# In-product transposes and projections, and a PSUM-seeded last block product, in the final stage of a decoder trunk

## The chip, the cores and the metric

The kernel runs on one core of one Trainium2 chip. The metric is the device time of one execution in microseconds (us), lower is better. The time before is 1259.64 us, the median of three runs (1259.33 to 1259.81).

The core's engines, as the profile names them: PE (TensorE, matrix products and transposes; PEld is its weight load), DVE (VectorE), ACT (ScalarE), POOL (GpSimd) and SP (SyncE, which here only issues DMAs). Each engine works through its own queue of instructions in order. SBUF is the working memory; PSUM holds the results of PE in eight banks of 128 x 512 f32 values.

## The reference

Two decoder layers over 512 tokens of width 1024. Each ends with a per-layer embedding, and the change lies in that of the second layer, the last stage of the whole computation:

```python
def _per_layer_embedding(x, p_i, norm, w_gate, w_proj):
    gate = jax.nn.sigmoid(_rms_norm(x, norm) @ w_gate)
    return gate * (p_i @ w_proj)
...
        x = x + _conv_ffn(_rms_norm(x, ffn_norm[i]), ffn_w_up[i], ffn_conv_w[i], ffn_conv_b[i], ffn_w_down[i])
        x = x + _per_layer_embedding(x, p[i], ple_norm[i], ple_w_gate[i], ple_w_proj[i])
    return x
```

Here `w_gate` is 1024 x 1024, `p_i` is 512 x 256 and `w_proj` is 256 x 1024. All values are float32.

## The kernel before

**Layout.** The residual `x` is held transposed, as eight tiles `xT[m]` of 128 channels x 512 tokens. Products in float32 accuracy are made of three passes of a reduced form: each operand is split into a high and a low part, and high x high, high x low and low x high are added up in a PSUM bank (`mm3`, L156 to L158, and in the last stage L889 to L891). ACT makes the high part with a copy (L100, L136, L868) and DVE the low part with a subtraction (L101, L137, L869).

**PSUM.** Two groups of four banks: `ps` (for the large products) and `pa` (for everything small: transposes, projections, norm sums). Tiles are handed out from a pool, and a tile's bank is free again when its last reader is done.

**Order of work.** A planner orders the instructions of each engine by readiness and program order. Inside `tc.manual_schedule(...)`, in `ple1`, the instructions of PE, DVE and ACT keep the order in which they are written.

**The last stage.** `ffn(1, ...)` ends with the down projection. For each of its eight output tiles `done` adds the residual (L767), and `blocks` (L254) prepares, for pairs of tiles, the left operands of the next product: the gate product of `x` (512 x 1024) with `w_gate` (1024 x 1024) is done as a two-by-two block product with seven block products instead of eight, so `blocks` forms sums and differences of the blocks of `x` (`e1`, `o1`, `o2`, `s1` to `s4`), and `minus` (L875) forms differences of the weight blocks `b11`, `b12`, `b22`, `b21`. The squares of `x` are summed into `acc` (L248 to L252). `end_norm` (L290) turns `acc` into the scale `r` per token: four small matmuls against ones (L296), a DVE step (`rs`, L165) and a power on POOL (L166).

`ple1` (L843) then runs the block products in the order e1, s1, s2, s3, s4, o2, o1. One block product (`add`, L880) is 24 matmuls: 4 blocks j of the inner dimension x 2 token tiles i x 3 passes, into two banks. The banks `X` hold e1, then e1 + s2, then e1 + s2 + s3 and so on; `Q` holds s1, later s1 + s4. Values that are needed again later are copied to SBUF by ACT (`ka`: the result of e1; `kd`: s1; `kb`: e1 + s2) and added by DVE when a quadrant of the result is complete (`summed`, L925). `chunk` (L861) splits a half of a weight block into its high and low part for `add`; the names are wt1, wt2, wt3, wt4, w22, w21 and, for `w_proj`, wj.

For each quadrant of the output (a pair of token tiles t by a column half hf) there are three steps outside the block products:

- `back(hf, t)` (L893): four PE transposes of `xT` into a `pa` bank, and an ACT copy to SBUF;
- `proj(t, w)` (L908): six matmuls p x w_proj into a `pa` bank;
- `finish(hf, t, ...)` (L930): ACT takes the sigmoid, scaled by `r`, of the gate (L933), DVE multiplies it with the projection in its `pa` bank (L934) and adds the residual (L935), and SP issues the store (L936).

These steps stand between the block products: before s2, after s2, after s3, after s4 and after o2. In the last product, o1, the three result banks (one whole token tile and two halves of the other) are each summed with `ka` by DVE before the sigmoid (L995 to L1005).

The weights and `p` of this stage are loaded by DMAs on SP's queue while the down projection still runs.

Of the kernel before, what the change touches and what calls it, by code (L numbers as in the profile page):

```python
# [13 lines left out]
AF = mybir.ActivationFunctionType  # L14
# [7 lines left out]
NT = S // P  # L22
# [33 lines left out]
class Kernel:  # L56
# [658 lines left out]
    def ffn(self, i, next_gain):  # L715
        nc, a, tc = self.nc, self.a, self.tc
        xg, R = self.xg, None
        wu = a["ffn_w_up"][i].rearrange("(k p) n -> p k n", p=P)
        w0, w1, w2, bb = self.fcv
        with tc.tile_pool(name=f"ffn{i}", bufs=1) as fp:  # L720
            acts = [self.pair(self.fp, "b0", "b1") for f in range(8)]
            for f in range(8, NF, 2):
                four = self.four(fp)
                acts += [(four[:, 0], four[:, 1]), (four[:, 2], four[:, 3])]

            def taps(ps, f):
                y = fp.tile([P, S], F32, tag="zt", name=self.nm("zt"), bufs=4)
                z = fp.tile([P, S + 2], F32, tag="z", name=self.nm("z"), bufs=3)
                nc.gpsimd.memset(z[:, :2], 0.0)
                nc.vector.tensor_tensor(z[:, 2:], ps, R, ALU.mult)  # L730
                nc.scalar.activation(y, z[:, 2:], AF.Identity, scale=w2[:, f : f + 1], bias=bb[:, f : f + 1])  # L731
                for tap, w in ((1, w1), (0, w0)):
                    nc.vector.scalar_tensor_tensor(  # L733
                        out=y, in0=z[:, tap : tap + S], scalar=w[:, f : f + 1], in1=y, op0=ALU.mult, op1=ALU.add
                    )
                return y

            for d in range(NF // 2):
                wg = self.weights(wu[:, :, 256 * d : 256 * d + 256], ND, 256)
                wv = self.weights(wu[:, :, DFF + 256 * d : DFF + 256 * d + 256], ND, 256)  # L740
                for c in range(2):
                    f = 2 * d + c
                    got = []
                    pss = []
                    for w in (wg, wv):
                        ps = self.ps()
                        for k in range(ND):
                            self.mm3(ps, w(k, c * P, (c + 1) * P), xg[k], start=k == 0, stop=k == ND - 1)
                        pss.append(ps)
                    if R is None:  # L750
                        R = self.spread()
                    for w, ps, fo in ((wg, pss[0], f), (wv, pss[1], NF + f)):
                        y = taps(ps, fo)
                        if w is wg:
                            nc.scalar.activation(y, y, AF.Gelu)  # L755
                        got.append(y)
                    g, y = got
                    nc.vector.tensor_tensor(y, g, y, ALU.mult)  # L758
                    self.split(acts[f], y)
            self.begin_norm(("a0", "a1"))  # L760
            done = self.residual(next_gain)
            if i == 1:
                self.forms = []
                scratch = lambda: fp.tile([P, S], F32, tag="zt", name=self.nm("gx"), bufs=4)

                def done(m, ps):
                    nc.vector.tensor_tensor(self.xT[m], self.xT[m], ps, ALU.add)  # L767
                    self.blocks(m, next_gain, scratch)

            self.project(self.rows(a["ffn_w_down"][i]), acts, ND, done)  # L770
            self.end_norm()
            if i == 1:
                self.ple1(fp)

    def p_halves(self, i):
# [67 lines left out]
    def ple1(self, fp):  # L843
# [1 line left out]


        nc, a, tc = self.nc, self.a, self.tc
        r, forms = self.r, self.forms
        wg = a["ple_w_gate"][1].rearrange("(j u p) n -> u p j n", p=P, u=2)
        wp = a["ple_w_proj"][1].rearrange("(k p) n -> p k n", p=P)  # L850
        sl = lambda hl, t: (hl[0][:, t * P : (t + 1) * P], hl[1][:, t * P : (t + 1) * P])
        H, J = D // 2, ND // 2
# [8 lines left out]
        def chunk(src):  # L861
            if count[0] % 6 < 3:
                h, l = (self.wp.tile([P, 2, H], F32R, tag=g, name=self.nm(g), bufs=3) for g in ("wh", "wl"))
            else:
                four = self.four(fp)
                h, l = four[:, :2], four[:, 2:]
            count[0] += 1
            nc.scalar.activation(h, src, AF.Copy)  # L868
            nc.vector.tensor_tensor(l, src, h.bitcast(F32), ALU.subtract)  # L869
            return h, l  # L870

        def chunks(raw):
            return [chunk(raw[:, 2 * q : 2 * q + 2, :]) for q in range(2)]

        def minus(out, x, y):  # L875
            for q in range(2):
                c = slice(2 * q, 2 * q + 2)
                nc.vector.tensor_tensor(out[:, c, :], x[:, c, :], y[:, c, :], ALU.subtract)  # L878
# [46 lines left out]
        def summed(g, kept):  # L925
            s = result()[:, : g.shape[1]]
            nc.vector.tensor_tensor(s, g, kept, ALU.add)
            return s

        def finish(hf, t, g, x, pj, s=None, c0=0, c1=H):  # L930
            if s is None:
                s = result()[:, c0:c1]
            nc.scalar.activation(s, g, AF.Sigmoid, scale=r[:, t : t + 1])  # L933
            nc.vector.tensor_tensor(s, s, pj[:, c0:c1], ALU.mult)  # L934
            nc.vector.tensor_tensor(s, s, x[:, c0:c1], ALU.add)  # L935
            nc.sync.dma_start(self.out[0, t * P : (t + 1) * P, hf * H + c0 : hf * H + c1], s)  # L936

        ET = mybir.EngineType
        b11 = block(0, 0, True)
# [4 lines left out]
        wj_raw = self.four(fp, F32)  # L944
# [2 lines left out]
        proj_load(0)  # L947
        minus(b11, b12, b11)
        wt1 = [chunk(b11[:, :2, :])]
        X = [self.ps() for _ in range(2)]  # L950
        with tc.manual_schedule(engines={ET.PE, ET.DVE, ET.Activation}):
            add(X, "e1", w11, first=True)
            wt1.append(chunk(b11[:, 2:, :]))
            minus(b11, b22, b11)
            ka = [self.sp.tile([P, S], F32, tag=g, name=self.nm("keep"), bufs=n) for g, n in (("acc", 1), ("sq", 2))]
            for k, x in zip(ka, X):
                nc.scalar.copy(k, x)
            pT = self.load_p(1, fp, pin)
            wt2 = chunks(b11)
            wj = chunk(wj_raw[:, 2:, :])  # L960
            Q = [self.ps() for _ in range(2)]
            add(Q, "s1", wt1, first=True)
            minus(b12, b22, b12)
            kd = keep(Q, "R")
            wt3 = chunks(b12)
            xs = [back(1, t) for t in (2, 3)]
            add(X, "s2", wt2)
            kb = [self.sp.tile([P, S], F32, tag="sq", name=self.nm("keep"), bufs=2), result()]
            for k, x in zip(kb, X):
                nc.scalar.copy(k, x)  # L970
            pjs = [proj(t, wj) for t in (2, 3)]
            w22 = chunks(b22)
            minus(b11, b21, b11)
            wt4 = [chunk(b11[:, :2, :])]
            add(X, "s3", wt3)
            ss = [summed(X[t], kd[t]) for t in (0, 1)]
            for t in (0, 1):
                finish(1, t + 2, ss[t], xs[t], pjs[t], ss[t])
            xs = [back(1, t) for t in (0, 1)]
            pjs = [proj(t, wj) for t in (0, 1)]  # L980
            wt4.append(chunk(b11[:, 2:, :]))
            wj = chunk(wj_raw[:, :2, :])
            add(Q, "s4", w22)
            ss = [summed(Q[t], kb[t]) for t in (0, 1)]
            for t in (0, 1):
                finish(1, t, ss[t], xs[t], pjs[t], ss[t])
            xs = [back(0, t) for t in (2, 3)]
            pjs = [proj(t, wj) for t in (2, 3)]
            w21 = chunks(b21)
            add(X, "o2", wt4)  # L990
            for t in (0, 1):
                finish(0, t + 2, X[t], xs[t], pjs[t])
            xs = [back(0, t) for t in (0, 1)]
            pjs = [proj(t, wj) for t in (0, 1)]
            Y = [self.ps() for _ in range(3)]  # L995
            halves = ((0, H // 2), (H // 2, H))

            add(None, "o1", w21, first=True, order=[(j, 0, (0, H), Y[0]) for j in range(J)])
            s = summed(Y[0], ka[0])
            finish(0, 0, s, xs[0], pjs[0], s)  # L1000
            for y, c in zip(Y[1:], halves):
                y = y[:, : H // 2]
                add(None, "o1", w21, first=True, order=[(j, 1, c, y) for j in range(J)])
                s = summed(y, ka[1][:, c[0] : c[1]])
                finish(0, 1, s, xs[1], pjs[1], s, *c)  # L1005


    def mixer1(self):
# [450 lines left out]
```

## Time and profile before

| What | Value |
|---|---|
| Median of three runs | 1259.64 us |
| The profiled execution, whole | 1259.64 us |
| Its span in the profile | 1257.8 us |
| Instructions | 14849 |
| Mean granted clock of TensorE | 0.998 |
| Start of e1, first matmul of the last stage | 1191.20 us |
| First matmul of s1 / s2 / s3 / s4 / o2 / o1 | 1198.89 / 1205.24 / 1213.50 / 1226.47 / 1236.55 / 1245.82 us |
| Start of the last matmul | 1251.29 us |
| End of the last add on DVE | 1255.21 us |

Times in the profile count from the start of the span; what lies between the span and the whole time (1.84 us) is outside it. A row of a timeline gives the start, the duration, the engine, the line of the kernel, the operation, output <- inputs by their names, shapes and, in brackets, how long the engine sat idle before it and who released it. Rows with xN are several instructions of one kind in a row. Matmuls overlap, so the time that each takes of PE is the distance between starts and not the listed duration. The granted clock is 1.00 at full speed.

### The profile page before, as it was taken

The page shows a single profiled execution, that of the slowest core. Times are in us where ns is not written, and L with a number is a line of the kernel's source. Part 1 is how long each engine was busy: PE and PEld are TensorE (multiplying, and loading weights), DVE is VectorE, ACT ScalarE, POOL GpSimd, SP SyncE. Part 2 cuts the span into 40 slices and gives each one's busy share as a digit, 9 for nine tenths or more (in the row PEclk, how much of TensorE's full clock was granted, in tenths as well). Part 3 has the DMA queues.
Part 4 walks back from the last instruction along what each step waited for, and adds up shares of the span by engine and source line. Part 5 has one row for each costly group of instructions (what it writes and reads, how often), then busy time and mean ns, then how long its engine had stood idle before and what let it go on. Part 6 is the DMA issues. An engine that isn't in the chain of part 4 may idle for free.

```text
span 1257.8 us, 14849 instructions
## 1 busy us (share of the span) xinstructions
PE 1240.0 (99%) x5809; PEld 1031.0 (82%) x5809; DVE 800.6 (64%) x1230; ACT 559.2 (44%) x864; POOL 54.8 (4%) x150
## 2 busy tenths in 40 slices
PE   7999999999999999999999999999999999999997
PEld 7877788888888888888989988888888888888876
DVE  6786556777777633346779665557777777344584
ACT  6466344444444322234564544435444444233362
POOL 2500000000000000000100000000000000000000
PEclk9999999999999999999999999999999999999999
DMA  6221332223332222232322212233333222333401
GB/s 212 74 96 49 89 101 79 90 100 101 101 101 101 92 92 92 92 101 92 108 73 66 89 46 74 94 109 101 101 101 100 88 85 97 101 102 107 167 17 51
DMA packets 111002, 117.42 MB, mean 93 GB/s; under 512 B 2728, under 2 KB 106210, under 8 KB 110932
## 3 DMA queue, kind: packets, MB, share of 16 engines
q1 hardware_dynamic: 109568, 115.35, 27.9%
q0 software_dynamic: 560, 0.42, 0.2%
q8 instruction: 45, 0.74, 0.2%
q10 hardware_dynamic: 804, 0.70, 0.2%
q14 instruction: 25, 0.20, 0.1%
HBM read 114.37 MB, written 2.10 MB: 93 GB/s over the span
## 4 chain that ended last, share of the span: by engine, by line
PE 91%; DVE 4%; ACT 2%; issue 2%; POOL 1%; DMA 1%; SPq 0%; DVEq 0%; ACTq 0%; POOLq 0%
PE ps L156 27%; PE ps L157 27%; PE ps L158 27%; PE pa L1179 1%; PE pa L156 1%; DMA xin<-in_x_dram 1%; PE pa L1293 1%; PE pa L157 1%; PE pa L158 0%; DVE wl L137 0%; DVE raw L878 0%; PE pa L1270 0%; PE pa L541 0%; POOL rq L166 0%; PE pa L588 0%
## 5 line engine op out<-in xcount | busy, mean ns | idle before, releaser
L136 ACT ACTIVATE wh<-raw 128x1024 fp32r<-128x1024 f32 (+4 forms) x212 | 214.4, 1013 | 349.0 <-PE ps L157 300.3
L137 DVE TENSOR_TENSOR wl<-raw,wh 128x1024 fp32r<-128x1024 f32 (+4 forms) x212 | 246.7, 1165 | 160.6 <-ACT wh L136 159.6
L156 PE MATMUL ps<-a,wh 128*128 128x512 f32 x864 | 337.1, 390 | 0.0
L157 PE MATMUL ps<-a,wh 128*128 128x512 f32 x864 | 336.7, 390 | 0.0
L158 PE MATMUL ps<-a,wl 128*128 128x512 f32 x864 | 336.5, 389 | 0.0
L156 PEld LDWEIGHTS ps<-a,wh 128*128 128x128 f32 x864 | 162.2, 188 | 34.1 <-issue 0.7
L157 PEld LDWEIGHTS ps<-a,wh 128*128 128x128 f32 x864 | 162.3, 188 | 33.9 <-issue 0.3
L158 PEld LDWEIGHTS ps<-a,wl 128*128 128x128 f32 x864 | 162.2, 188 | 33.6
L733 DVE SCALAR_TENSOR_TENSOR zt<-z,vfa,zt 128x512 f32<-128x512 f32 x176 | 131.4, 749 | 3.6 <-ACT zt L731 0.6
L156 PE MATMUL ps<-b,wh 128*128 128x512 f32 x320 | 126.5, 396 | 0.5 <-ACT b L100 0.5
L158 PE MATMUL ps<-b,wl 128*128 128x512 f32 x320 | 125.3, 392 | 0.0
L157 PE MATMUL ps<-b,wh 128*128 128x512 f32 x320 | 125.0, 391 | 0.0
L730 DVE TENSOR_TENSOR z<-ps,R 128x512 f32<-128x512 f32 x88 | 60.4, 688 | 74.7 <-PE ps L158 74.7
L157 PE MATMUL ps<-four,wh 128*128 128x512 f32 x224 | 87.2, 389 | 0.0
L156 PE MATMUL ps<-four,wh 128*128 128x512 f32 x224 | 87.2, 389 | 0.0
L158 PE MATMUL ps<-four,wl 128*128 128x512 f32 x224 | 87.2, 389 | 0.0
L731 ACT ACTIVATE zt<-z,vfb 128x512 f32<-128x512 f32 x88 | 70.8, 807 | 5.1 <-DVE z L730 3.3
L156 PEld LDWEIGHTS ps<-b,wh 128*128 128x128 f32 x320 | 60.0, 188 | 13.9 <-ACT b L100 1.3
L158 PEld LDWEIGHTS ps<-b,wl 128*128 128x128 f32 x320 | 60.1, 188 | 12.5
L157 PEld LDWEIGHTS ps<-b,wh 128*128 128x128 f32 x320 | 60.1, 188 | 12.2
L755 ACT ACTIVATE zt<-zt 128x512 f32<-128x512 f32 x44 | 27.8, 631 | 74.8 <-DVE zt L733 74.8
L100 ACT ACTIVATE four<-zt 128x512 fp32r<-128x512 f32 x28 | 17.7, 632 | 77.4 <-DVE zt L758 77.4
(347 smaller groups left out, 1566.5 us busy)
## 6 DMA issues: line engine op xcount, KB each, us to landing
raw<-in_ffn_w_up_dram SPq DMA_DIRECT2D x44, 1024.0 KB, 5.0
raw<-in_ffn_w_down_dram SPq DMA_DIRECT2D x16, 1024.0 KB, 5.1
raw<-in_hy_w_in_dram SPq DMA_DIRECT2D x8, 1024.0 KB, 4.9
raw<-in_gla_w_in_dram SPq DMA_DIRECT2D x8, 1024.0 KB, 5.3
raw<-in_ffn_w_down_dram SPq DMA_DIRECT2D x8, 768.0 KB, 4.3
raw<-in_ple_w_gate_dram SPq DMA_DIRECT2D x6, 1024.0 KB, 5.1
raw<-in_gla_w_out_dram SPq DMA_DIRECT2D x4, 1024.0 KB, 5.1
raw<-in_gla_w_in_dram SPq DMA_DIRECT2D x4, 672.0 KB, 4.0
```

The source lines that it names most:

```text
L100: nc.scalar.activation(h, src, AF.Copy)
L136: nc.scalar.activation(hv, v, AF.Copy)
L137: nc.vector.tensor_tensor(lv, v, hv.bitcast(F32), ALU.subtract)
L156: mm(out, lh, rh, start=start, stop=False)
L157: mm(out, lh, rl, start=False, stop=False)
L158: mm(out, ll, rh, start=False, stop=stop)
L730: nc.vector.tensor_tensor(z[:, 2:], ps, R, ALU.mult)
L731: nc.scalar.activation(y, z[:, 2:], AF.Identity, scale=w2[:, f : f + 1], bias=bb[:, f : f + 1])
L733: nc.vector.scalar_tensor_tensor(out=y, in0=z[:, tap : tap + S], scalar=w[:, f : f + 1], in1=y, op0=ALU.mult, op1=ALU.add)
L755: nc.scalar.activation(y, y, AF.Gelu)
L1179: mm(second(pl[:, c], b), F[:, c], second(F[:, c], b), start=True, stop=True)
L1293: mm(po, sc[:, c], vt[j][:, h * GDV : (h + 1) * GDV], start=True, stop=j == 0)
```

## The change

The norm of the second layer's embedding moves from the end of `ffn` into the hand-written order, behind the first two steps of s1. The transposes and projections move into the block products: s1, s2, s4 and o2 are cut in two parts, and `back` and `proj` run between the parts (for o1: between its first bank and its two halves). wj is prepared behind wt3 instead of ahead of s1. A sigmoid of `r` with an unused result stands ahead of s3. In the last product, ACT copies `ka` into the PSUM banks that o1 will use (parts of `Q` and `X`, no banks of their own any more), o1's matmuls add to what is there, and the sigmoid reads the bank; the three DVE sums are gone. `self.r` is read in `finish` where `r` was.

```diff
@@ ffn
             self.project(self.rows(a["ffn_w_down"][i]), acts, ND, done)
-            self.end_norm()
-            if i == 1:
+            if i == 0:
+                self.end_norm()
+            else:
                 self.ple1(fp)
...
@@ ple1, finish
-            nc.scalar.activation(s, g, AF.Sigmoid, scale=r[:, t : t + 1])
+            nc.scalar.activation(s, g, AF.Sigmoid, scale=self.r[:, t : t + 1])
...
-        X = [self.ps() for _ in range(2)]
+        X, Q = [[self.ps() for _ in range(2)] for _ in range(2)]
+        both = (0, H)
         with tc.manual_schedule(engines={ET.PE, ET.DVE, ET.Activation}):
             add(X, "e1", w11, first=True)
             wt1.append(chunk(b11[:, 2:, :]))
             minus(b11, b22, b11)
+            steps = [(j, i, both, Q[i]) for j in range(J) for i in range(2)]
+            add(None, "s1", wt1, first=True, order=steps[:2])
+
+            self.end_norm()
             ka = [self.sp.tile([P, S], F32, tag=g, name=self.nm("keep"), bufs=n) for g, n in (("acc", 1), ("sq", 2))]
             for k, x in zip(ka, X):
                 nc.scalar.copy(k, x)
+            wt2 = chunks(b11)
             pT = self.load_p(1, fp, pin)
-            wt2 = chunks(b11)
-            wj = chunk(wj_raw[:, 2:, :])
-            Q = [self.ps() for _ in range(2)]
-            add(Q, "s1", wt1, first=True)
+            add(None, "s1", wt1, order=steps[2:])
             minus(b12, b22, b12)
             kd = keep(Q, "R")
             wt3 = chunks(b12)
+            wj = chunk(wj_raw[:, 2:, :])
+            steps = [(j, i, both, X[i]) for j in range(J) for i in range(2)]
+            add(None, "s2", wt2, order=steps[:4])
             xs = [back(1, t) for t in (2, 3)]
-            add(X, "s2", wt2)
+            add(None, "s2", wt2, order=steps[4:])
...
             wt4 = [chunk(b11[:, :2, :])]
+            nc.scalar.activation(self.few(NT, "rlo"), self.r, AF.Sigmoid)
             add(X, "s3", wt3)
             ss = [summed(X[t], kd[t]) for t in (0, 1)]
             for t in (0, 1):
                 finish(1, t + 2, ss[t], xs[t], pjs[t], ss[t])
+            steps = [(j, i, both, Q[i]) for j in range(J) for i in range(2)]
+            add(None, "s4", w22, order=steps[:6])
             xs = [back(1, t) for t in (0, 1)]
             pjs = [proj(t, wj) for t in (0, 1)]
             wt4.append(chunk(b11[:, 2:, :]))
             wj = chunk(wj_raw[:, :2, :])
-            add(Q, "s4", w22)
+            add(None, "s4", w22, order=steps[6:])
             ss = [summed(Q[t], kb[t]) for t in (0, 1)]
+
+            halves = ((0, H // 2), (H // 2, H))
+            Y = [Q[0]] + [y[:, : H // 2] for y in (Q[1], X[0])]
             for t in (0, 1):
                 finish(1, t, ss[t], xs[t], pjs[t], ss[t])
+            nc.scalar.copy(Y[0], ka[0])
+            nc.scalar.copy(Y[1], ka[1][:, : H // 2])
+            steps = [(j, i, both, X[i]) for j in range(J) for i in range(2)]
+            add(None, "o2", wt4, order=steps[:6])
             xs = [back(0, t) for t in (2, 3)]
             pjs = [proj(t, wj) for t in (2, 3)]
             w21 = chunks(b21)
-            add(X, "o2", wt4)
+            add(None, "o2", wt4, order=steps[6:])
             for t in (0, 1):
                 finish(0, t + 2, X[t], xs[t], pjs[t])
+                if t == 0:
+                    nc.scalar.copy(Y[2], ka[1][:, H // 2 :])
+            add(None, "o1", w21, order=[(j, 0, both, Y[0]) for j in range(J)])
             xs = [back(0, t) for t in (0, 1)]
             pjs = [proj(t, wj) for t in (0, 1)]
-            Y = [self.ps() for _ in range(3)]
-            halves = ((0, H // 2), (H // 2, H))
-
-            add(None, "o1", w21, first=True, order=[(j, 0, (0, H), Y[0]) for j in range(J)])
-            s = summed(Y[0], ka[0])
-            finish(0, 0, s, xs[0], pjs[0], s)
+            finish(0, 0, Y[0], xs[0], pjs[0])
             for y, c in zip(Y[1:], halves):
-                y = y[:, : H // 2]
-                add(None, "o1", w21, first=True, order=[(j, 1, c, y) for j in range(J)])
-                s = summed(y, ka[1][:, c[0] : c[1]])
-                finish(0, 1, s, xs[1], pjs[1], s, *c)
+                add(None, "o1", w21, order=[(j, 1, c, y) for j in range(J)])
+                finish(0, 1, y, xs[1], pjs[1], None, *c)
```

More of the change, by code (lines that the diff above doesn't have):

```diff
@@ L847, in ple1 @@
         nc, a, tc = self.nc, self.a, self.tc
-        r, forms = self.r, self.forms
+        forms = self.forms
         wg = a["ple_w_gate"][1].rearrange("(j u p) n -> u p j n", p=P, u=2)
```

## The prediction

> **What bounds the kernel now.** I read the page first: the busy shares and the chain that ended last.
>
> ```profile
> PE 1240.0 (99%) x5809; PEld 1031.0 (82%) x5809; DVE 800.6 (64%) x1230; ACT 559.2 (44%) x864; POOL 54.8 (4%) x150
> PE 91%; DVE 4%; ACT 2%; issue 2%; POOL 1%; DMA 1%; SPq 0%; DVEq 0%; ACTq 0%; POOLq 0%
> ```
>
> TensorE (PE) is the bound, so only time in which PE stands still or runs slowly, and time after its last matmul, can be won. The diff touches only the end of the kernel, so next come busy times by stretch there.
>
> ```profile
> 1196.60:1251.40 54.80, 51.65 (x253) 42.98 (x252) 36.76 (x43) 26.14 (x36) 1.92 (x1) 0.97 0.08 30
> ...
> 1219.00:1222.00 3.00, 0.98 (x9) 0.74 (x7) 1.50 (x3) 2.70 (x4) 0.00 (x0) 1.00 0.00 0
> 1222.00:1225.50 3.50, 3.42 (x8) 2.75 (x9) 3.43 (x6) 2.77 (x4) 0.00 (x0) 0.51 0.33 130
> ```
>
> Columns: stretch, length, busy PE, PEld, DVE, ACT, POOL, then the granted clock, DMA share and GB/s. From the end of product e1 to the last matmul is 54.8 us. Within it PE does little for 3 us at 1219, and for the 3.5 us after that its clock is 0.51. The waits of PE in the stage, and its own timeline, say why:
>
> ```profile
> PE pa L156 <- DVE so L934: 2.8, 2, 2.1
> PE pa L296 <- DVE acc L252: 0.4, 1, 0.4
> ```
>
> ```profile
> 1196.41 0.39 PE L891 MATMUL ps<-wh,b 128*128 128x512 f32 x1
> 1197.15 1.05 PE L296 MATMUL pa<-ones,acc 128*128 128x1 f32 x8 [0.35 <-DVE acc L252]
> 1198.07 1.07 PE L795 MATMUL pa<-cf,pin 128*128 128x128 f32 x8
> 1198.89 0.48 PE L889 MATMUL ps<-wh,a 128*128 128x512 f32 x1
> ...
> 1218.94 1.04 PE L897 MATMUL pa<-cf,xT 128*128 128x128 f32 x8
> 1222.08 0.79 PE L156 MATMUL pa<-wh,four 128*128 128x512 f32 x1 [2.09 <-DVE so L934]
> ...
> 1226.47 0.40 PE L889 MATMUL ps<-four,a 128*128 128x512 f32 x1
> ...
> 1233.68 0.50 PE L156 MATMUL pa<-wh,four 128*128 128x512 f32 x1 [0.70 <-DVE so L934]
> ...
> 1251.29 0.28 PE L891 MATMUL ps<-four,b 128*128 128x256 f32 x1
> ```
>
> Back-to-back matmuls start 0.2265 us apart (23 steps from 1213.50 to 1218.71 in product s3); their listed 0.39 overlaps. PE loses four times: (a) e1's last slot ends at 1196.64, and the norm's matmuls start at 1197.15: 0.51. (b) At 1218.94 the eight transposes of two `back` take a mean 0.885 (the two clean groups: 1204.45 to 1205.24, 1241.99 to 1242.97), so PE is free at 1219.83 and starts the projection at 1222.08: 2.25. It needs a `pa` bank, of which there are four, and the one whose turn it is holds the projection that finish(1, 2) multiplies at L934. (c) The 12 matmuls of that projection then take 4.39 (1222.08 to 1226.47) against 12 x 0.2265 = 2.72: 1.67 for the low clock. (d) The same bank wait again, 1232.83 to 1233.68: 0.85. Together 5.28.
>
> The tail, from the timelines of DVE and ACT:
>
> ```profile
> 1250.94 0.69 DVE L935 TENSOR_TENSOR so<-so,xt 128x512 f32<-128x512 f32 x1
> 1251.55 0.42 DVE L927 TENSOR_TENSOR so<-ps,keep 128x256 f32<-128x256 f32 x1
> ...
> 1252.54 0.42 DVE L934 TENSOR_TENSOR so<-so,pa 128x256 f32<-128x256 f32 x1 [0.57 <-ACT so L933]
> 1253.00 0.42 DVE L935 TENSOR_TENSOR so<-so,xt 128x256 f32<-128x256 f32 x1
> 1253.34 0.42 DVE L927 TENSOR_TENSOR so<-ps,keep 128x256 f32<-128x256 f32 x1
> 1253.79 0.51 ACT L933 ACTIVATE so<-so,rtok 128x256 f32<-128x256 f32 x1 [1.28 <-DVE so L927]
> 1254.33 0.42 DVE L934 TENSOR_TENSOR so<-so,pa 128x256 f32<-128x256 f32 x1 [0.57 <-ACT so L933]
> 1254.79 0.42 DVE L935 TENSOR_TENSOR so<-so,xt 128x256 f32<-128x256 f32 x1
> ```
>
> The last matmul starts at 1251.29, but its sum (L927) starts only at 1253.34, behind the previous half's multiply and add in DVE's queue. The last add ends at 1255.21: 3.92 after the last matmul's start; the store takes the rest of the span.
>
> **The change, part by part.** The sum is made for PE from 1196.64 on; all matmuls and transposes stay, only their order changes.
>
> Norm behind six matmuls of s1. They need wt1[0], ready at 1193.80, and run 1196.64 to 1198.00; `acc` is ready at 1197.10, so wait (a) goes: -0.51. Norm (0.92, to 1198.92), p transposes (0.82, to 1199.74) and 18 matmuls of s1 (0.09 for the first after a transpose, 0.32 against 0.23, and 4.08) end at 1203.91. The norm's release of `acc` comes 0.85 later, and ACT's two keeps (0.96) with it, to 1200.05.
>
> Order of wj. DVE is full here and wj's low part is now last. From 1197.61: wt1 1.13, two subtractions 2.27, rs 0.08, wt2 2.27, pT 1.20, two subtractions 2.27, wt3 2.27, wj 1.22, all from the rows of before, end at 1210.3. ACT's part of each fits in front (wt2's first: 1200.05 + 1.05 = 1201.10, DVE is there at 1201.09). PE: s2's 12, two `back` (0.885), 0.09, s2's 12 reach the projection at 1210.32. Bounds: 0 if DVE is as quick as that, 0.8 if its seven changes of partner each cost another 0.1 (a dependent start trails its releaser by 0.03 to 0.1 in the timelines). I take 0.2, near the low end because most of DVE's operations wait for nothing.
>
> Transposes and projection after 18 of s4's 24 matmuls. With s3 from 1213.2 to 1218.7, the 18 run to 1222.74, the transposes to 1223.6, and only then is the `pa` bank wanted. It comes free with L934: s3's first bank is done about 1218.2, then sum 0.69, sigmoid 0.73, multiply 0.69 and starts between: 1220.5. So 3.1 us of cover; (b) and with it (c) go: -2.25 - 1.67. The same after 18 of o2 (bank wanted 1232.8, free about 1230.2): -0.85. In o1 it is wanted at 1240.6 and free at 1237.9.
>
> Sigmoid on r ahead of s3. It pulls the table load (1.28 in before, on the path behind the sum) into ACT's 1.94 us of idle time before it: 1.28 + 0.21 (a 128x4 activation) fits. Without that cover the multiply is late by under 1.3, inside the 3.1 above. Nothing extra.
>
> Weights prepared later in ACT's and DVE's queues: wt4[1] ready about 1226.5, used at 1230.5; w21's halves ready 1235.5 and 1236.7, used at 1236.9 and 1238.3. If that 1.4 is used up, o1 waits one for one.
>
> Seeds in PSUM: three ACT copies replace three DVE sums. No row of before has ACT writing PSUM; bounds are a 128x128 ACT operation reading it (0.36) and the 128x1024 one in SBUF (1.06); I take the 0.61 of the 128x512 copy out of PSUM. The first two come about 1230, behind them wait the copies of the `back` at 1232.3, so 2 us hide them even at 1.06 each. Matmuls that add to a bank have the same 0.2265 as those that start one (s2 against s1).
>
> Tail: the last half goes from matmul to sigmoid without a sum. Matmul 0.28, start 0.04, then the steps of before from sigmoid to add: 1252.00 to 1252.54, to 1253.00, + 0.42 = 1.42. So 1.74 instead of 3.92: -2.18. The first half's add is over by then, 0.5 before.
>
> PE's total: 180 x 0.2265 = 40.77, 24 halves x 0.1196 = 2.87, norm 0.92, p 0.82, four pairs of `back` 3.54, five first matmuls 0.45, wj 0.2: 49.57 against 54.77, -5.2. The queue of stores on SP only moves up. With the tail -7.4: span 1257.8 - 7.4 = 1250.4. The profiled execution took 1259.64 (1.84 around the span), which is the median, so **1252.2 us**.
>
> [...]
>
> **Rivals.**
> B, the planner's order: norm and its `rs` leave the part in front of the hand-written order, so block DVE work (wt1 and two subtractions, 3.4 us) could be placed ahead of the last `acc` add. Then `acc` is ready at 1200.5, PE stands 2.5 us after its six matmuls, and as at (b) the clock falls: +1.67, less the 0.2 at wj: 1256.2. For: ACT's half of wt1 already ran early, at 1192.14. Against: DVE was full up to 1197.61 with older work.
> C, the tail keeps its length: finish(0, 0) is late and its multiply and add stand before the halves. +2.2: 1254.4. Against: sigmoid by 1242, multiply and add by 1243.5, the first half's sum only at 1244.9.
> D, no gain: each of the five transpose groups inside a product costs 1.5 us more than its 0.885, by waits for banks or weights that I have hidden: 1259.6. Against: covers of 1.4 to 3.1.
> [...]
>
> **How the numbers follow.** My forecast 0.74, B 0.10, C 0.05, D 0.04, E 0.07. A change under 0.2% (2.5 us) is about what can't be told from none; A, B and C are faster by more: 0.89, D is the same: 0.04, E slower: 0.07. The range runs from 1250.9 (wj free, `back` at 0.79 each time, and 0.7 of starts saved) to B's 1256.2.
>
> **What would show it.** Right: PE's six L889 to L891 before L296 without a wait; no wait for L934; clock 1.00 throughout; the last add 1.7 after the last matmul's start; first sigmoid without the table load. Wrong: a wait of L156 for L869 above 0.8 at about 1210, any stretch near clock 0.5, or a wait in front of the norm.

## The result and the profile after

The changed kernel takes 1251.93 us (median of 6 runs, 1251.36 to 1252.46) against 1259.59 us before (6 runs, 1259.33 to 1259.81). The ratio is 0.9939, 95% interval 0.9927 to 0.9952: faster by 7.7 us, and the forecast was 1252.2. The span of the profiled execution is 1250.0 us in place of 1257.8.

The changed kernel's page, its busy shares and its chain that ended last:

```profile
PE 1237.4 (99%) x5809; PEld 1029.8 (82%) x5809; DVE 799.0 (64%) x1227; ACT 560.8 (45%) x868; POOL 55.0 (4%) x150
PE 94%; DVE 2%; issue 1%; ACT 1%; POOL 1%; DMA 1%; SPq 0%; DVEq 0%; POOLq 0%
```

PE has as many instructions as before; its share of the chain went from 91% to 94%, DVE's from 4% to 2%: what was won is time in which PE waited for others. The busy times by stretch, columns as before:

```profile
1196.60:1246.50 49.90, 49.37 (x253) 41.55 (x251) 37.12 (x44) 28.64 (x42) 1.93 (x1) 1.00 0.10 38
1219.00:1222.00 3.00, 3.00 (x15) 2.49 (x14) 2.82 (x5) 1.12 (x2) 0.00 (x0) 1.00 0.07 27
1222.00:1225.50 3.50, 3.50 (x22) 2.97 (x21) 0.46 (x2) 2.31 (x4) 0.00 (x0) 1.00 0.36 131
```

The stretch at 1219, where PE did 0.98 us of work in 3, is full, and the one after it, at clock 0.51 before, is at 1.00. The changed kernel's timeline of PE shows where the moved work went, and where the one new wait is:

```profile
1197.71 0.39 PE L892 MATMUL ps<-wh,a 128*128 128x512 f32 x1
1197.94 0.95 PE L296 MATMUL pa<-ones,acc 128*128 128x1 f32 x8
1198.74 1.07 PE L796 MATMUL pa<-cf,pin 128*128 128x128 f32 x8
1199.57 0.48 PE L890 MATMUL ps<-wh,a 128*128 128x512 f32 x1
...
1210.10 0.39 PE L156 MATMUL pa<-wh,four 128*128 128x512 f32 x1
1210.40 0.50 PE L157 MATMUL pa<-wl,four 128*128 128x512 f32 x1
...
1222.55 1.03 PE L898 MATMUL pa<-cf,xT 128*128 128x128 f32 x8
1223.34 0.48 PE L156 MATMUL pa<-wh,four 128*128 128x512 f32 x1
```

The norm (L296) starts right behind six matmuls of s1, with no wait in brackets. The transposes inside s4 take 0.79, and the projection follows them at once (L156 at 1223.34). At 1210.10 a projection starts and its second matmul, the first to read wj's low part, is 0.07 late and the third another 0.11: the new wait, 0.18.

The end of the kernel, from its timeline over all engines:

```profile
1245.69 0.28 PE L892 MATMUL ps<-four,b 128*128 128x256 f32 x1
...
1246.01 0.47 ACT L934 ACTIVATE so<-ps,rtok 128x256 f32<-128x256 f32 x1 [0.96 <-PE ps L892]
1246.52 0.42 DVE L935 TENSOR_TENSOR so<-so,pa 128x256 f32<-128x256 f32 x1 [0.55 <-ACT so L934]
1246.97 0.42 DVE L936 TENSOR_TENSOR so<-so,xt 128x256 f32<-128x256 f32 x1
```

The sigmoid reads the bank as soon as the last matmul is out, and the last add ends 1.70 us after that matmul's start, against 3.92 before.

### The profile page after: what moved, and what is told of

The parts are those of the page before. It is cut to its first block, busy times and chain, and to the rows that moved or that the text cites. A ratio compares the mean times of both kernels' runs of the same rounds, so it can differ in the third digit from the quotient of the medians.

```text
span 1250.0 us, 14845 instructions
## 1 busy us (share of the span) xinstructions
PE 1237.4 (99%) x5809; PEld 1029.8 (82%) x5809; DVE 799.0 (64%) x1227; ACT 560.8 (45%) x868; POOL 55.0 (4%) x150
## 4 chain that ended last, share of the span: by engine, by line
PE 94%; DVE 2%; issue 1%; ACT 1%; POOL 1%; DMA 1%; SPq 0%; DVEq 0%; POOLq 0%
PE ps L156 28%; PE ps L158 27%; PE ps L157 27%; PE pa L1192 1%; PE ps L892 1%; PE ps L890 1%; PE ps L891 1%; PE pa L157 1%; PE pa L1306 1%; PE pa L156 1%; PE pa L158 1%; DMA xin<-in_x_dram 1%; DVE wl L137 0%; PE pa L1283 0%; PE pa L541 0%
## 5 line engine op out<-in xcount | busy, mean ns | idle before, releaser
L156 PE MATMUL ps<-a,wh 128*128 128x512 f32 x864 | 336.9, 390 | 0.0
L156 PEld LDWEIGHTS ps<-a,wh 128*128 128x128 f32 x864 | 162.2, 188 | 33.9 <-issue 0.7
L156 PE MATMUL ps<-b,wh 128*128 128x512 f32 x320 | 126.5, 396 | 0.5 <-ACT b L100 0.5
L156 PE MATMUL ps<-four,wh 128*128 128x512 f32 x224 | 87.1, 389 | 0.0
L156 PEld LDWEIGHTS ps<-b,wh 128*128 128x128 f32 x320 | 60.0, 188 | 13.9 <-ACT b L100 1.3
```

What stands on the lines that cost most here:

```text
L156: mm(out, lh, rh, start=start, stop=False)
```

## The experiments

Single times of one kernel differ by one to two us, because the work ahead of the last stage does: e1 started between 1190.67 and 1192.69 in the profiles of these runs. Inside the last stage the profiles agree to some hundredths, so the readings rest on two lengths: **stage**, from e1's first matmul to the start of the last matmul, and **tail**, from there to the end of the last add. The medians stand beside them (before, run beside them: 1259.41, 1259.57 and 1259.51 in the three batches). "Wait" is PE's wait for a `pa` bank behind s3.

| Kernel | stage | tail | wait | clock after it | median, ratio to before (95%) |
|---|---|---|---|---|---|
| before | 60.09 | 3.92 | 2.09 | half | 1259.59 |
| after | 54.56 | 1.70 | none | full | 1251.93, 0.9939 (0.9927 to 0.9952) |
| sigmoid_early_alone | 57.25 | 3.94 | 0.76 | full | 1256.31, 0.9977 (0.9968 to 0.9986) |
| seeds_alone | 58.52 | 1.70 | 2.09 | full | 1256.60, 0.9983 (0.9973 to 0.9992) |
| sums_ahead | 60.16 | 2.53 | 2.09 | half | 1257.93, 0.9990 (0.9981 to 1.0000) |
| inserts_alone | 54.61 | 2.55 | none | full | 1253.10, 0.9953 (0.9938 to 0.9968) |
| no_early_sigmoid | 54.57 | 1.70 | none | full | 1252.32, 0.9943 (0.9928 to 0.9958) |
| s4_whole | 55.55 | 1.71 | 0.70 | full | 1252.33, 0.9944 (0.9927 to 0.9960) |
| s4_whole_no_sigmoid | 58.47 | 1.70 | 2.04 | half | 1256.17, 0.9973 (0.9964 to 0.9983) |
| norm_first | 55.08 | 1.70 | none | full | 1252.36, 0.9945 (0.9930 to 0.9960) |
| wait_longer_by_3 | 56.03 | 1.70 | 1.17 | full | 1252.77, 0.9946 (0.9933 to 0.9960) |
| wait_longest | 56.17 | 1.70 | 1.33 | full | 1253.96, 0.9956 (0.9942 to 0.9969) |
| seeds_and_sigmoid | 57.23 | 1.69 | 0.72 | full | 1254.73, 0.9961 (0.9946 to 0.9976) |
| smaller_last_piece | 56.30 | 1.33 | none | full | 1253.64, 0.9954 (0.9941 to 0.9966) |

### The wait behind s3: the early sigmoid alone

Before, with one line:

```diff
+            nc.scalar.activation(self.few(NT, "rlo"), self.r, AF.Sigmoid)
             add(X, "s3", wt3)
```

> The kernel before with one line added: the unused sigmoid of r ahead of s3. Theory: the table load (1.28 us) leaves the path from the sum of s3 to the multiply that frees the bank, so PE's wait after s3 falls from 2.25 to about 0.95; as the wait of 0.85 after s4 left the clock at full speed, this one does too, and the 1.67 us of half clock goes: 1259.6 - 1.3 - 1.7 = 1256.6. Rival: any wait at this place lets the clock fall, so only the load is won: 1258.3. Second rival: the table load is paid elsewhere on the path: 1259.6.

The stage shortened by 2.84. Waits of PE in this kernel's last stage:

```profile
PE pa L156 <- DVE so L934: 1.5, 2, 0.8
PE pa L296 <- DVE acc L252: 0.4, 1, 0.4
```

The two waits for a bank are 1.5 us together in place of 2.8, the longer one 0.76, and the clock stayed at full speed behind it. So the table load (1.28 us in before) was on the path, and the low clock was a consequence of it: a wait of 0.76 did not bring it, one of 2.09 can. The rival that any wait lowers the clock falls, and so does the one that the load is paid elsewhere on the path.

### The wait behind s3: s4 uncut, with and without the early sigmoid

After, with back and proj between s3 and s4 again; the second kernel also leaves out the line of the early sigmoid:

```diff
-            add(None, "s4", w22, order=steps[:6])
             xs = [back(1, t) for t in (0, 1)]
             pjs = [proj(t, wj) for t in (0, 1)]
...
-            add(None, "s4", w22, order=steps[6:])
+            add(None, "s4", w22, order=steps)
```

> The changed kernel with back and proj of token tiles 0 and 1 between s3 and s4 again, s4 uncut; the early sigmoid stays. Theory: PE waits about 0.9 us for the bank (back done at 1219.3, multiply done at 1220.2), and that is too short to lower the clock: 1251.9 + 0.9 = 1252.8. Rival: the clock falls for any wait here: +2.6, 1254.5.

> As s4_whole, and without the early sigmoid: the place as it was before the change, all else changed. Theory: wait 2.2 and half clock for 3.4 us again: 1251.9 + 2.2 + 1.7 = 1255.8, granted clock near 0.5 after the wait. Rival: the wait without the low clock: 1254.1.

Against after, the stages are 0.99 and 3.91 longer; 0.9 and 3.9 were expected. The second one's busy times (1221.90 to 1226.00) and its PE timeline:

```profile
1221.90:1226.00 4.10, 3.60 (x10) 2.90 (x11) 4.03 (x6) 3.19 (x5) 0.00 (x0) 0.66 0.34 127
```

```profile
1222.40 0.50 PE L156 MATMUL pa<-wh,four 128*128 128x512 f32 x1 [2.04 <-DVE so L935]
1222.73 0.39 PE L157 MATMUL pa<-wl,four 128*128 128x512 f32 x1
1222.96 0.42 PE L158 MATMUL pa<-wh,four 128*128 128x512 f32 x1
1223.19 0.61 PE L156 MATMUL pa<-wh,four 128*128 128x512 f32 x1
1223.61 0.63 PE L157 MATMUL pa<-wl,four 128*128 128x512 f32 x1
```

The wait of 2.04 is back and so is the low clock (0.66 on average here), but not at once: after the wait two matmuls still follow each other at 0.23, and only from 1223.19 on are they 0.42 apart. In these profiles either the early sigmoid or the cut of s4 by itself removes the low clock; the cut also removes what is left of the wait.

### The early sigmoid where s4 is cut

After, with that one line left out.

> The changed kernel without the unused sigmoid of r. Theory: the table load goes back behind the sum of s3, the multiply that frees the bank is 1.3 us later (about 1221.5), still ahead of the projection inside s4 at 1223.3, so nothing changes: 1251.9, no wait of PE there. Rival: the load delays the path of s4 after all: 1253.2.

Stage 54.57 against 54.56, no wait of PE: with s4 cut, the line is worth nothing. The two edits overlap, and the gains of edits that are tried one at a time on before must not be added.

### The tail: the seeds alone, and the order of DVE alone

Before with the seeds of o1 (Y in parts of Q and X, three ACT copies, matmuls that add, no sums), the transposes and projections left between the products:

```diff
-            add(None, "o1", w21, first=True, order=[(j, 0, (0, H), Y[0]) for j in range(J)])
-            s = summed(Y[0], ka[0])
-            finish(0, 0, s, xs[0], pjs[0], s)
+            add(None, "o1", w21, order=[(j, 0, (0, H), Y[0]) for j in range(J)])
+            finish(0, 0, Y[0], xs[0], pjs[0])
...
-                s = summed(y, ka[1][:, c[0] : c[1]])
-                finish(0, 1, s, xs[1], pjs[1], s, *c)
+                finish(0, 1, y, xs[1], pjs[1], None, *c)
```

> The kernel before with only the last product seeded in PSUM (three ACT copies, no DVE sums in o1), transposes and projections between the products as before. Theory: the tail from the last matmul's start to the last add shortens from 3.92 to about 1.74 us and nothing else changes: 1259.6 - 2.2 = 1257.4. Rival: without the transposes and projections inside o1, finish(0, 0) still stands in DVE's queue ahead of the halves, so only the sum itself (0.4 to 0.5) and part of the queue is won: 1258.3 to 1259.1.

And before with nothing but another order of DVE's instructions in o1 (`late` holds the arguments of the piece before; for the whole token tile its sigmoid is issued first and `ended` does the multiply, add and store):

```diff
                 s = summed(y, ka[1][:, c[0] : c[1]])
-                finish(0, 1, s, xs[1], pjs[1], s, *c)
+                finish(*late) if late[1] else ended(*late[:2], *late[3:])
+                late = (0, 1, s, xs[1], pjs[1], s, *c)
+            finish(*late)
```

> The kernel before with the order of DVE alone changed in o1: each half's sum stands ahead of the multiply and add of the piece before it; no seeds. Theory: most of the long tail is the queue on DVE and not the sums: the last add ends about 1253.85 instead of 1255.21, so 1259.6 - 1.4 = 1258.2. Rival: the sum itself is the cost; the order gives nothing: 1259.6, or a little more, as the last half's multiply comes later.

The seeds shorten the tail to 1.70, the whole 2.22 without help from the moved transposes; their rival falls. (Its median is 0.8 below its theory: in its profile the clock stayed up behind the wait of 2.09, which is taken up below.) The order alone shortens it to 2.53, by 1.39. DVE's timeline in that kernel:

```profile
1251.65 0.42 DVE L927 TENSOR_TENSOR so<-ps,keep 128x256 f32<-128x256 f32 x1
1251.98 0.41 DVE L934 TENSOR_TENSOR so<-so,pa 128x256 f32<-128x256 f32 x1
1252.43 0.42 DVE L935 TENSOR_TENSOR so<-so,xt 128x256 f32<-128x256 f32 x1
1252.77 0.41 DVE L934 TENSOR_TENSOR so<-so,pa 128x256 f32<-128x256 f32 x1
1253.22 0.42 DVE L935 TENSOR_TENSOR so<-so,xt 128x256 f32<-128x256 f32 x1
```

The last sum (L927) now stands ahead of the previous half's multiply and add, and while ACT takes its sigmoid, DVE does these. So 1.39 of the 2.22 was the queue on DVE; only the other 0.83 needed the sums to go.

### The moves without the seeds

After, with the sums of before in o1 (its banks started afresh, `ka` added by DVE).

> The changed kernel without the seeds: o1 starts its banks afresh and DVE adds ka, as before. Theory: PE's 5.2 us stay won. The tail has the sum again, but finish(0, 0) is over before the halves end, so it is 0.45 (the sum) plus about 0.4 (queued behind the first half's add) longer than with seeds: 1251.9 + 0.9 = 1252.8. Rival: the seeds are worth their whole 2.2 of the sum, so that the parts add: 1254.1.

Stage as after (54.61), tail 2.55, that is 0.85 longer than after. The parts don't add in the tail: with finish(0, 0) done early, the sums cost 0.85 and not 2.22.

### The two cheap parts together

Before with the seeds and the early sigmoid, nothing moved into a product:

> The kernel before with the seeds of o1 and the early sigmoid, nothing moved into a product and the norm where it was. Theory: the two do not touch each other, so their gains add: by the profiles 2.2 for the tail and 2.85 (1.3 of waiting, 1.55 of half clock) at the wait, 1259.5 - 5.05 = 1254.4, and what is left to the changed kernel are the waits of 0.76, 0.70 and 0.51 and the first matmuls behind them: 2.5. Rival: with the shorter waits the seeds' copies or w21 come too late and o1 waits: over 1255.5.

Stage shorter by 2.86, tail by 2.23: 5.09 of the 7.75 that the changed kernel wins by the same two lengths (5.53 + 2.22). The moves into the products, with the new places of the norm and of wj, add the 2.67 that is left of the stage: waits of 0.72, 0.70 and 0.36 as PE's timeline lists them, a little more each by distance of starts, and slow starts behind them.

### The norm's place

After, with `end_norm` ahead of s1's first six matmuls in place of behind them:

> The changed kernel with the norm's four matmuls ahead of s1's first six instead of behind them. Theory: PE waits about 0.5 us for the sum of squares again, no more: 1252.4. Rival: ACT's keeps and with them wt2 come earlier, DVE's chain to wj ends earlier, and part of it is won back at the projection after s2: 1252.1 to 1252.2.

Stage 0.52 longer; the 0.35 wait for `acc` is back in its timeline. The rival was half right: the wait at wj is gone, 0.18, but the norm and the transposes of p, now apart, make PE change once more from small f32 work to the product (0.32 in place of 0.23 at 1198.43 and again at 1200.70); the norm's own matmuls also take 0.91 in place of 0.80. So the gain is not seen in the sum.

### How long a wait lowers the clock

`s4_whole` and `s4_whole_no_sigmoid` with three and four small unused sigmoids of the first sum ahead of finish(1, 2):

```diff
+            for _ in range(3):
+                nc.scalar.activation(self.few(NT, "rlo"), ss[0][:, :NT], AF.Sigmoid)
             for t in (0, 1):
                 finish(1, t + 2, ss[t], xs[t], pjs[t], ss[t])
```

> As s4_whole, with three small unused sigmoids of the first sum (0.21 us each) ahead of finish(1, 2) on ACT, so that PE's wait for the bank after s3 is about 1.35 us in place of 0.70. Theory, from s4_whole (0.70, clock kept) and from the wait of 2.1, after which the clock fell in some executions and not in others: whether it falls is chance and more likely the longer PE stands, so at 1.35 it falls seldom or never: 1251.9 + 1.0 + 0.65 = 1253.5, all executions within some 0.5 of each other. Rival: a wait above about 1 us is enough for it to fall each time: 1255.2.

> As s4_whole_no_sigmoid, with four such sigmoids, so that PE waits about 2.9 us in place of 2.0. Theory: now the clock falls in every execution: 1256.2 + 0.85 = 1257.0, with none lower by 1.7. Rival: the fall has nothing to do with the length, some executions keep the clock: about one in four near 1255.3.

The first waited 1.17 us and kept the clock, and its four times lie within 0.8: the rival falls. It is quicker than expected because three such sigmoids took 0.44 together and not 0.63. The second is inconclusive on its question: its wait is 1.33 and not 2.9, as ACT's timeline says:

```profile
1218.16 1.28 ACT L985 ACT_TABLE_LOAD   x1
1220.27 0.54 ACT L985 ACTIVATE rlo<-so 128x4 f32<-128x4 f32 x4 [0.83 <-DVE so L928]
1220.90 1.33 ACT L934 ACTIVATE so<-so,rtok 128x512 f32<-128x512 f32 x2
```

Ahead of the small sigmoids the table load ran at 1218.16, before the sum was ready; ahead of finish's own sigmoid, in s4_whole_no_sigmoid, it started at 1219.61, when the sum was done. Why the load waits in one place and not in the other is not settled here. The run says only that at 1.33 the clock is kept too. Its four times lie in two pairs, at 1252.84 and 1252.96 and at 1254.95 and 1254.97. The traced execution is of the upper pair and kept the clock; its e1 started at 1192.69, the latest of all profiles.

### A smaller last piece

After, with wj prepared ahead of wt3's second half, and the last half of o1 in two pieces of 128 columns:

```diff
-            wt3 = chunks(b12)
-            wj = chunk(wj_raw[:, 2:, :])
+            wt3 = [chunk(b12[:, :2, :])]
+            wj = chunk(wj_raw[:, 2:, :])
+            wt3.append(chunk(b12[:, 2:, :]))
...
-            for y, c in zip(Y[1:], halves):
+            parts = [(Y[1], halves[0])] + [(Y[2][:, q : q + P], (H // 2 + q, H // 2 + q + P)) for q in (0, P)]
+            for y, c in parts:
```

> The changed kernel with wj prepared ahead of wt3's second half, and o1's last half cut in two pieces of 128 columns. Theory: no wait of PE at the projection after s2 (-0.2), and the steps behind the last matmul are shorter (sigmoid by 0.1, multiply and add by 0.13 each, -0.35), if the 24 small matmuls take the 1.43 us that the 12 took: 1251.4, visible in the profile, hardly in the times. Rival: a matmul of 128 columns is held up by its weight load (0.19 listed, every 0.12 at best seen here), the 24 take 2.9 in place of 1.43: 1252.8.

The tail is 1.33, 0.37 shorter as forecast, and PE no longer stops at wj. But the stage is 1.74 longer. From its timeline of PE:

```profile
1244.55 0.22 PE L890 MATMUL ps<-wh,a 128*128 128x128 f32 x1
...
1245.72 0.28 PE L892 MATMUL ps<-four,b 128*128 128x128 f32 x1
1246.51 0.33 PE L890 MATMUL ps<-wh,a 128*128 128x128 f32 x1 [0.51 <-ACT so L934]
...
1247.79 0.28 PE L892 MATMUL ps<-four,b 128*128 128x128 f32 x1
```

A matmul of 128 columns takes 0.106 on average (11 steps from 1244.55 to 1245.72) where one of 256 takes 0.12, so each piece of 12 costs almost as much as a whole half. And the second piece lies in the same bank as the first and waits until ACT has read that one. The 24 matmuls cost 1.1 more (24 x 0.106 against 12 x 0.12), the bank 0.7 (1245.72 to 1246.51, less one step), wj gives 0.2 back: 1.6 of the 1.74. The rival came near for the matmuls (2.5 against its 2.9; that the weight load is the reason is not shown), and it missed the bank. That the order of wj is worth its 0.2 was not tried by itself.

## Why the prediction was right

By its own steps, forecast against what the profiles show:

- **(a) Norm:** -0.51 forecast; taken back, it costs 0.52, the wait of 0.51 and small terms that cancel. The norm starts at 1197.94, forecast 1198.00.
- **wj:** 0.2 forecast, 0.18 measured, and it goes when wj is prepared earlier.
- **(b) and (c), s4:** 2.25 and 1.67 forecast; put back, 3.91. The bank was free at 1220.16 (end of L935's first multiply: 1219.47 + 0.69) and wanted at 1223.34: 3.2 of cover, forecast 3.1.
- **(d), o2:** 0.85 forecast. No wait is left there; it wasn't tried by itself, and sits in the 2.67 above.
- **Early sigmoid:** forecast as nothing extra; it is nothing where s4 is cut. But as the experiments show, that one line would have won 2.84 of (b) and (c) by itself, which the working did not say, although it had the table load on the path.
- **Weights:** wt4[1] ready at 1226.48 (forecast 1226.5), w21's halves at 1235.60 and 1236.73 (1235.5 and 1236.7). No wait.
- **Seeds in PSUM:** 0.61 taken for a copy of 128 x 512, measured 0.58, and 0.36 and 0.38 for the 256-column ones; all hidden.
- **Tail:** -2.18 forecast, -2.22 measured. The prediction put it down to the sum and the queue together; the queue is 1.39 of it.
- **PE's total:** 49.57 forecast, 49.23 measured (1196.58 to 1245.69 and one last slot of 0.12). The mis-sized term is the pairs of `back`: 0.885 was a mean with the 0.98 at 1241.99, and each takes 0.79 to 0.80, as the other row had it. Four times 0.09 is 0.36. The norm's matmuls took 0.80 (1197.94 to 1198.74) where the sum had 0.92, another 0.12, and late starts of a few hundredths behind the transposes and in the projections give 0.14 back: 0.34.

What it had wrong in kind is the certainty of (c). The 1.67 was counted as paid in every execution. In the seeds-alone kernel the same wait left the clock alone; its PE timeline and its busy times:

```profile
1221.95 0.50 PE L156 MATMUL pa<-wh,four 128*128 128x512 f32 x1 [2.09 <-DVE so L934]
1222.29 0.40 PE L157 MATMUL pa<-wl,four 128*128 128x512 f32 x1
1222.53 0.39 PE L158 MATMUL pa<-wh,four 128*128 128x512 f32 x1
```

```profile
1221.90:1226.00 4.10, 4.05 (x18) 3.36 (x19) 4.03 (x5) 2.75 (x4) 0.00 (x0) 1.00 0.35 130
```

Its stage is 58.52 where before has 60.09, 1.57 less, with the same waits. The fall came in three of the four profiled executions with a wait of this length, so the change removes a loss that is not paid every time. What the records of the clock show of it is told in the last section.

Rivals: B did not come (DVE did the last `acc` add at 1196.35, ahead of the second half of wt1 at 1197.55). C did not come: finish(0, 0) was done at 1243.25, the first half's sigmoid started at 1244.58. D did not come: each cut cost the 0.79 of its transposes and some 0.09 for the first matmul behind them, both of them in the forecast's sum. E (slower, 0.07), a fall of the clock at each group of small matmuls inside a product, did not come: the clock was 1.00 throughout the stage (1196.60 to 1246.50), with five such groups.

## What to carry to other kernels

When the bound engine waits, look at how long each wait is and what follows it: here a wait of 2.1 us cost another 1.6 us in low clock in three of four profiles, and shortening it to 0.76 with a table load moved into idle time did away with that. A queue in order can hold the last result: putting the last sum ahead of older, less urgent work on DVE gave 1.39 us with no other change, so order is worth trying before the arithmetic is rebuilt. Edits that remove the same wait overlap, so take one out of the finished version as well as adding it to the old one before saying what it is worth.

## What the runs showed of the hardware

**The fall of the clock is not fixed by the wait.** Four profiled executions had the wait of 2.04 to 2.09 us behind s3: in before, sums_ahead and s4_whole_no_sigmoid the clock fell (0.72 on average from 1221 to 1227 in each), in seeds_alone it did not (1.00), and in s4_whole_no_sigmoid it fell only after PE had been at work again for 0.8 us (1222.40 to 1223.19). Behind waits of 0.70 to 1.33 at the same place it stayed up in all five profiled kernels (1.00 from 1221 to 1227).

The records of the granted clock say when it changed. In before the first record at full clock starts at 13.67 (matmuls of 256 columns start 0.21 apart ahead of that and 0.12 behind it); the clock is at half from 1221.99, back at 1225.40, 3.41 later, and at half again from 1256.12, after the last matmul. In after the first record at full clock starts at 13.45, and the clock falls once, at 1249.07, after the last matmul. From the start of the first record to the falls it is 1208.32 and 1242.45 us in before and 1235.63 in after, which is 354, 364 and 362 times 3.413.

These are stretches of 3.41 us in the four executions with the long wait:

```profile
1218.58:1221.99 3.41, 1.40 (x11) 1.03 (x9) 1.91 (x4) 2.69 (x4) 0.00 (x0) 1.00 0.00 0
1218.53:1221.94 3.41, 1.32 (x11) 0.99 (x9) 1.89 (x4) 2.88 (x4) 0.00 (x0) 1.00 0.00 0
1219.79:1223.20 3.41, 1.37 (x10) 1.00 (x9) 1.94 (x4) 3.40 (x6) 0.00 (x0) 1.00 0.00 0
1218.41:1221.82 3.41, 1.45 (x11) 1.08 (x9) 1.92 (x4) 2.65 (x4) 0.00 (x0) 1.00 0.00 0
```

They are of before, sums_ahead, s4_whole_no_sigmoid and seeds_alone, columns as before. In the first three PE was busy for 1.32 to 1.40 us of the 3.41, and behind the stretch the clock was low: by the records in before, and by the matmuls, which start 0.42 to 0.43 apart from 1222.36 on in sums_ahead and from 1223.19 on in s4_whole_no_sigmoid. In seeds_alone PE was busy for 1.45 in a stretch that ends 0.13 ahead of the end of its wait (1221.82 and 1221.95), and the clock stayed up; no fall marks the end of that stretch, and its place, 354 steps of 3.413 behind the start of the first record as in before, is the author's estimate. In before and after, counted in steps of 3.413 from the start of the first record, three stretches at full clock have 1.4 us of PE work or less (1.4 and 0 in before, 0.3 in after), and the clock fell at the end of each; the other 722 at full clock have 2.27 or more, and at the end of none did it fall. An estimate from before's 1.40 and the 1.45 of seeds_alone is that a single wait brought the fall where it covered some 2.0 of such a 3.41 us (3.41 - 1.4). The waits of 0.70 to 1.33, which kept the clock, are shorter than that; those of 2.04 to 2.09 are just long enough if nearly all of it lies in one stretch. Nothing here shows why the steps are of 3.41 us, or why the fall came at 1.40 and not at 1.45.

The times of before may have the same cause: of 52 runs, 12 lie at 1257.2 to 1258.1 (median 1257.6) and 40 at 1258.9 to 1261.7 (median 1259.6), and none between. The distance of 2.0 is near the 1.67 of half clock. That the lower group are the executions without the fall is not shown: one execution of each kernel has a trace, and the two pairs of wait_longest are 2.0 apart too, with the clock at 1.00 from 1216 to 1227 in the traced execution of the upper pair. There the late start of e1 may make part of the distance.
